# A bidirectional scan's masks in one instruction, its state split at the step's beginning, and the attention gates' SiLU moved into the attention

## The chip, the cores and the metric

One core of a Trainium2 chip runs the whole layer as one program. The metric is the device time of one execution in microseconds (us); smaller is better. The engines are TensorE (PE; PEld is its weight load), VectorE (DVE), ScalarE (ACT), GpSimd (POOL) and SyncE (SP), which issues the transfers here. Each engine takes its instructions in order.

## The reference, cut to what matters

Two sequences, of 512 and 1024 tokens and width 1024, go through one encoder layer. The normalised, modulated input is multiplied by a wide matrix; its columns feed an attention branch and a state-space branch.

```python
branch_a = (attn * jax.nn.silu(gate_a)) @ w_proj_a          # attn: 8 heads, softmax over the sequence
...
CB = jnp.einsum('bclgn,bcsgn->bcgls', Cc, Bc)               # per chunk of 128 and group
Lm = jnp.exp(jnp.where(tri, diff, -jnp.inf))                # decays between two tokens of a chunk
y_diag = jnp.einsum('bcgls,bcgels,bcsgep->bclgep', CB, Lm, xdt)
states = jnp.einsum('bclgn,bclge,bclgep->bcgepn', Bc, decay_states, xdt)
...
y = ssd(x, forward) + flip(ssd(flip(x), backward))          # both directions
merged = sigmoid(g_a) * branch_a + sigmoid(g_b) * (norm(y * silu(z)) @ w_proj_b)
out = x + gate * (merged @ w_out)
```

## The kernel before, in words

All arithmetic is float32. A product that needs precision is made of three matmuls on high and low halves (`mm3`, L88 to L90). A vector over tokens lies as 128 rows by 512 columns; the 1536 tokens are three such windows.

After a first stage (to about 200 us) the kernel goes through four groups `g` of the state-space branch. Each group makes its input projections and convolutions (PE-bound), then its scan, then the `z` gate. A scan is a pre-pass that carries the backward state from the last chunk to the first (`prepass`) and a main pass (`mainpass`) over the 4, then 8 chunks of 128 tokens of the two sequences. A chunk has two steps, `u` = 0 and 1, of four heads each. Between steps `feed` lets PE do parts of the fillers: other projections whose results are wanted later (`qc`, `gate`, `ga`, `gb`; `CUTS` says which group does which). The gate blocks are fillers of the first two groups. A filler's `ev` empties PSUM through ACT (for a gate, through DVE too) into `ft` and stores it.

In a main pass, `head(c)` fetches a chunk's inputs, makes the product of B and C in a PSUM tile `sm` (L651) and two masked copies `cu` of it, for the lower and the upper triangle (L653, L654). `distances` fetches the summed decays `ab`. `weights` subtracts on POOL (L714, two instructions), scales `cu` on ACT (L718, L719), adds (L720), merges the two directions (L721) and takes the exponential (L722). `weigh` multiplies (L727) and `products` does the matmuls (L738). `state` weights the chunk's inputs (L598) and splits them into halves on ACT and POOL (L688 to L691); `follow` multiplies those into the forward state (`mm3`, then L607 and L609). `carried` multiplies both states with C (L677) and scales the result (L678). `tail` adds all up (L743, L744). The PSUM pool `sm` has three slots, which `head`, `follow`, `carried` and the pre-pass take in turn.

The attention follows (about 1600 to 2187 us): 24 units of one head and one window. `scores` does the products of a unit ahead of time (maxima L1017 to L1022, exponentials L1025, whose results are `pp`), `values` transposes and multiplies (L1059, `po`). `gates` turns the sums of the softmax round through memory (`rsD`, `rb`), loads the stored gate `gt` (L1042) and multiplies (L1043); the last step multiplies it by the unit's result (L1072) and stores. `merge` interleaves the lists of these thunks. Fetched weights are cast on ACT (L361) and their low halves made on DVE (L85). The output products end the kernel.

The framework orders each engine's queue itself, from planned durations; the order of the program's text is the priority among the instructions that are ready in that plan.

Of the kernel before, what the change touches and what calls it, by code (L numbers as in the profile page):

```python
# [9 lines left out]
F32 = mybir.dt.float32  # L10
F32R = mybir.dt.float32r
U8 = mybir.dt.uint8
AF = mybir.ActivationFunctionType
ALU = mybir.AluOpType
# [4 lines left out]
P = 128  # L19
T = 1536  # L20
W = 512
# [44 lines left out]
def _body(nc, tc, A, O):  # L66
    V, S, GP, PE = nc.vector, nc.scalar, nc.gpsimd, nc.tensor
# [36 lines left out]
    cmat = const.tile([P, 5, P], F32, name="cmat")  # L104
    nc.sync.dma_start(out=cmat, in_=A["cmat"])
    maskb = const.tile([P, P], U8, name="maskb")
    ident, triF, triB, selL, selF = (cmat[:, i, :] for i in range(5))
# [406 lines left out]
    def filler(kind, i):  # L514
        if kind == "qc":
            def ev(w, ps):
                t = tmp("ft")
                S.copy(t, ps)
                nc.sync.dma_start(out=qcT[i][w], in_=t)
            return inproj_steps(i, ev)  # L520
        elif kind == "gate":
            def ev(w, ps):
                t = tmp("ft")
                S.activation(t, ps, AF.Tanh, scale=0.5)
                V.scalar_tensor_tensor(t, t, 1.0, ps, op0=ALU.add, op1=ALU.mult)
                nc.sync.dma_start(out=sgA[i][w], in_=t)
            return inproj_steps(BLK_GATE + i, ev)
        else:
            dst = tga if kind == "ga" else tgb

            def ev(w, ps):
                t = tmp("ft")
                S.activation(t, ps, AF.Tanh, scale=0.5)
                nc.sync.dma_start(out=dst[i][w], in_=t)
            return inproj_steps((BLK_GA if kind == "ga" else BLK_GB) + i, ev)
# [34 lines left out]
    for g in range(G):  # L570
# [61 lines left out]
        def mainpass(o, n):  # L632
# [5 lines left out]
            def head(c):  # L638
                cs_ = slice(c * P, (c + 1) * P)
                if c == c0:  # L640
                    xb = tok(c, "xb", 2)
                else:
                    xb = pS.tile([P, W + P], F32, name="xb", bufs=2)
                    nc.sync.dma_start(out=xb, in_=xbD[g][c])
                xt, bt = xb[:, :W], xb[:, W:]
                sb = None
                if c < c1 - 1:
                    sb = pS.tile([P, W], F32, name="sb", bufs=2)
                    nc.sync.dma_start(out=sb, in_=sbD[g][c])
                pc = smp.tile([P, P], F32, name="sm")  # L650
                PE.matmul(pc, lhsT=Bt[:, cs_], rhs=Ct[:, cs_], start=True, stop=True)  # L651
                cu = pS.tile([P, 2, P], F32, name="cu", bufs=2)
                V.tensor_tensor(cu[:, 0, :], pc, triF, op=ALU.mult)  # L653
                V.tensor_tensor(cu[:, 1, :], pc, triB, op=ALU.mult)  # L654
                stt[c] = dict(xt=xt, bt=bt, sb=sb, cu=cu)

            def decays(c):
                eb = {}
# [35 lines left out]
            def follow(c):  # L694
                stt[c]["sf"] = sf[0]
                if c < c1 - 1:
                    ps = smp.tile([P, W], F32, name="sm")
                    mm3(ps, *stt[c]["parts"], True, True)
                    sf[0] = advance(sf[0], ps, 0, c, pS.tile([P, W], F32, name="stf", bufs=2))
# [25 lines left out]
            def weigh(c, u):  # L725
                ab, wt = stt[c, u]
                V.tensor_tensor(wt, ab[:, 0], wt, op=ALU.mult)  # L727
                stt[c, u] = wt
# [16 lines left out]

            nu = E // HH
            us = [(c, u) for c in range(c0, c1) for u in range(nu)]
            head(c0)
            for i in range(4):
                xo = xs[i][:, o:o + n]  # L750
# [3 lines left out]
            weights(*us[0])  # L754
            yield
            for i in range(len(us) + 1):
                if i < len(us):
                    weigh(*us[i])
                if i + 2 < len(us):
                    distances(*us[i + 2])  # L760
                if i >= 1:
                    products(*us[i - 1])
                if i < len(us) and us[i][1] == 1:
                    follow(us[i][0])
                    carried(us[i][0])
                if i >= 1 and us[i - 1][1] == nu - 1:
                    tail(us[i - 1][0])
                if i + 1 < len(us):
                    weights(*us[i + 1])
                if i < len(us) and us[i][1] == 0:  # L770
                    c = us[i][0]
                    state(c)
                    decays(c)
                    if c + 1 < c1:
                        head(c + 1)
                yield
# [194 lines left out]
    def scores(u):  # L971

        si, hd, w = u
        o, n = SEQS[si]
        nw = n // W
        h = hd % 2
        st = {}

        def turn_n():
            qrw, qrr, rq, rqn = QR[si, hd // 2, w]  # L980
            nh = p2.tile([P, W], F32R, name="nh", bufs=2)
            nl = p2.tile([P, W], F32R, name="nl", bufs=2)
            pn = spp.tile([P, W], F32, name="sp")
            for b in range(4):
                PE.transpose(out=pn[:, b * P:(b + 1) * P], in_=qrw[:, b, h], identity=ident)
            S.activation(nh, pn, AF.Copy, scale=gqk)
            V.scalar_tensor_tensor(nl, pn, gqk, r32(nh), op0=ALU.mult, op1=ALU.subtract)
            st["n"] = (nh, nl)

        def turn_r():  # L990
            qrw, qrr, rq, rqn = QR[si, hd // 2, w]
            xh = p2.tile([P, W], F32R, name="xh", bufs=2)
            xl = p2.tile([P, W], F32R, name="xl", bufs=2)
            pk = spp.tile([P, W], F32, name="sp")
            for b in range(4):
                PE.transpose(out=pk[:, b * P:(b + 1) * P], in_=qrr[:, b, h], identity=ident)
            S.copy(xh, pk)
            sub(xl, pk, r32(xh))
            st["x"] = (xh, xl)
            PT[u] = []  # L1000
            st["su"] = p2.tile([P, nw, 4], F32, name="su", bufs=4)

        def block(b):
            (nh, nl), (xh, xl) = st["n"], st["x"]
            rq, rqn = QR[si, hd // 2, w][2:]
            bs = slice(b * P, (b + 1) * P)
            sm = p2.tile([P, 8], F32, name="smx", bufs=8)
            sps = []
            for k in range(nw):
                out = spp.tile([P, W], F32, name="sp")  # L1010
                kh, kl, kx = KV[si, hd, k][:3]
                PE.matmul(out, lhsT=nh[:, bs], rhs=kh, start=True, stop=False)  # L1012
                PE.matmul(out, lhsT=nh[:, bs], rhs=kl, start=False, stop=False)  # L1013
                PE.matmul(out, lhsT=nl[:, bs], rhs=kh, start=False, stop=False)  # L1014
                PE.matmul(out, lhsT=xh[:, bs], rhs=kx, start=False, stop=False)  # L1015
                PE.matmul(out, lhsT=xl[:, bs], rhs=kx, start=False, stop=True)  # L1016
                V.reduce_max(sm[:, k:k + 1], out, axis=AX.X)  # L1017
                sps.append(out)
            if nw == 2:
                V.scalar_tensor_tensor(sm[:, 2:3], sm[:, 0:1], sm[:, 1:2], rqn[:, b, h:h + 1], op0=ALU.max, op1=ALU.mult)  # L1020
            else:
                V.tensor_tensor(sm[:, 2:3], sm[:, 0:1], rqn[:, b, h:h + 1], op=ALU.mult)  # L1022
            pp = [p2.tile([P, W], F32, name="pp", bufs=10) for _ in range(nw)]
            for k in range(nw):
                S.activation(pp[k], sps[k], AF.Exp, bias=sm[:, 2:3], scale=rq[:, b, h:h + 1], accum_out=st["su"][:, k, b:b + 1])  # L1025
            PT[u].append(pp)

        def gates():

            su = st["su"]  # L1030
            if nw == 2:
                V.tensor_tensor(su[:, 0], su[:, 0], su[:, 1], op=ALU.add)
            V.reciprocal(su[:, 0], su[:, 0])
            pt = spp.tile([4, P], F32, name="sp")
            PE.transpose(out=pt, in_=su[:, 0], identity=ident)
            rt = p2.tile([4, P], F32, name="rt", bufs=2)
            S.copy(rt, pt)
            nc.sync.dma_start(out=rsD[hd][o // W + w].rearrange("(b q) -> b q", b=4), in_=rt)
            rb = p2.tile([P, W], F32, name="rb", bufs=1)
            nc.sync.dma_start(out=rb, in_=rsD[hd][o // W + w].partition_broadcast(P))  # L1040
            gt = p2.tile([P, W], F32, name="gt", bufs=1)
            nc.sync.dma_start(out=gt, in_=sgA[hd][o // W + w])  # L1042
            GP.tensor_tensor(gt, gt, rb, op=ALU.mult)  # L1043
            GT[u] = gt

        GT[u] = gates
        return [turn_n, turn_r], [lambda b=b: block(b) for b in range(4)]

    def values(u):

# [217 lines left out]
```

## Time and profile before

| | |
|---|---|
| median of 3 runs | 2720.13 us (2719.35 to 2723.41) |
| profiled execution | 2716.42 us |
| its span, first to last instruction | 2714.4 us |
| mean granted TensorE clock | 0.985 of full speed |
| four scans, in windows of 200 us each | 200 to 400, 560 to 760, 920 to 1120, 1320 to 1520 |
| attention | about 1600 to 2187 us |

The profile is one execution. "Busy" is the time in which an engine ran an instruction; matmuls overlap one another, so their single durations are longer than their spacing. A wait is put down to the instruction whose end released it.

### The profile page before, as it was taken

The page shows a single profiled execution, that of the slowest core. Times are in us where ns is not written, and L with a number is a line of the kernel's source. Part 1 is how long each engine was busy: PE and PEld are TensorE (multiplying, and loading weights), DVE is VectorE, ACT ScalarE, POOL GpSimd, SP SyncE. Part 2 cuts the span into 40 slices and gives each one's busy share as a digit, 9 for nine tenths or more (in the row PEclk, how much of TensorE's full clock was granted, in tenths as well). Part 3 has the DMA queues.
Part 4 walks back from the last instruction along what each step waited for, and adds up shares of the span by engine and source line. Part 5 has one row for each costly group of instructions (what it writes and reads, how often), then busy time and mean ns, then how long its engine had stood idle before and what let it go on. Part 6 is the DMA issues. An engine that isn't in the chain of part 4 may idle for free. (4 is left out here: it accounts for less than half of the span.)

```text
span 2714.4 us, 36314 instructions
## 1 busy us (share of the span) xinstructions
PE 2586.5 (95%) x12810; PEld 2080.5 (77%) x12810; DVE 1833.5 (68%) x2962; ACT 1322.6 (49%) x2954; POOL 505.1 (19%) x455
## 2 busy tenths in 40 slices
PE   6999999999999998999998999999999999999999
PEld 2776777877778766878766888888888788888887
DVE  5878785788946678557777568877777753466631
ACT  5545654456624456564556357666665651111210
POOL 1013440023400035110135024322222200000000
PEclk8999999999999999999999999999999999999999
DMA  7227662156722266542466322211110252255433
GB/s 249 77 78 208 187 168 94 39 179 187 207 62 86 82 208 183 136 147 74 146 191 188 92 96 87 84 44 43 34 40 28 71 186 70 78 156 163 128 125 101
DMA packets 211205, 325.86 MB, mean 120 GB/s; under 512 B 24816, under 2 KB 74064, under 8 KB 210256
## 3 DMA queue, kind: packets, MB, share of 16 engines
q1 hardware_dynamic: 211024, 323.55, 39.9%
q8 instruction: 101, 1.65, 0.3%
q14 instruction: 80, 0.66, 0.1%
HBM read 245.56 MB, written 77.91 MB: 119 GB/s over the span
## 5 line engine op out<-in xcount | busy, mean ns | idle before, releaser
L88 PE MATMUL mm<-hH,wh 128*128 128x512 f32 x1656 | 670.2, 405 | 2.3 <-ACT hH L218 2.0
L89 PE MATMUL mm<-hL,wh 128*128 128x512 f32 x1656 | 662.0, 400 | 3.6 <-DVE hL L219 3.6
L90 PE MATMUL mm<-hH,wl 128*128 128x512 f32 x1656 | 653.7, 395 | 1.3 <-DVE wl L85 1.2
L88 PEld LDWEIGHTS mm<-hH,wh 128*128 128x128 f32 x1656 | 314.6, 190 | 84.6 <-issue 14.6
L89 PEld LDWEIGHTS mm<-hL,wh 128*128 128x128 f32 x1656 | 315.4, 190 | 77.3 <-issue 10.2
L90 PEld LDWEIGHTS mm<-hH,wl 128*128 128x128 f32 x1656 | 314.6, 190 | 73.2 <-issue 6.1
L714 POOL TENSOR_TENSOR ab<-ab,dg 128x512 f32<-128x512 f32 x192 | 236.9, 1246 | 418.5 <-DMA ab<-arD 293.4
L88 PE MATMUL mm<-hi,wh 128*128 128x512 f32 x768 | 298.8, 389 | 0.0
L90 PE MATMUL mm<-hi,wl 128*128 128x512 f32 x768 | 298.8, 389 | 0.0
L89 PE MATMUL mm<-lo,wh 128*128 128x512 f32 x768 | 298.8, 389 | 0.0
L85 DVE TENSOR_TENSOR wl<-ws,wh 128x512 fp32r<-128x512 f32 x210 | 151.3, 722 | 134.4 <-ACT wh L226 86.7
L361 ACT CAST wh<-ws 128x512 fp32r<-128x512 f32 x72 | 44.9, 623 | 326.4 <-PE mm L89 311.3
L88 PEld LDWEIGHTS mm<-hi,wh 128*128 128x128 f32 x768 | 144.1, 188 | 30.1
L89 PEld LDWEIGHTS mm<-lo,wh 128*128 128x128 f32 x768 | 144.1, 188 | 29.9
L90 PEld LDWEIGHTS mm<-hi,wl 128*128 128x128 f32 x768 | 144.1, 188 | 29.9
L719 ACT ACTIVATE wt<-cu,dg 128x128 f32<-128x128 f32 x384 | 141.3, 391 | 46.5 <-DVE cu L653 46.1
L1025 ACT ACTIVATE pp<-sp,smx,rq 128x512 f32<-128x512 f32 x160 | 123.6, 777 | 54.9 <-DVE smx L1020 38.8
L361 ACT CAST ph<-tp 128x512 fp32r<-128x512 f32 x160 | 95.3, 598 | 110.4 <-PE tp L1059 110.2
L689 POOL TENSOR_TENSOR btl<-xb,bth 128x128 fp32r<-128x128 f32 x40 | 28.5, 713 | 607.5 <-ACT bth L688 607.4
L563 DVE SCALAR_TENSOR_TENSOR xs<-raw,cwh,xs 128x511 f32<-128x511 f32 (+3 forms) x128 | 129.7, 1021 | 17.5 <-ACT xs L559 14.8
L718 ACT ACTIVATE t<-cu,dg 128x128 f32<-128x128 f32 x384 | 137.3, 390 | 2.6 <-DVE cu L654 2.4
L721 DVE COPY_PREDICATED ab<-maskb,ab 128x512 f32<-128x512 uint8 x96 | 86.4, 905 | 69.3 <-POOL ab L714 69.3
(293 smaller groups left out, 5018.5 us busy)
## 6 DMA issues: line engine op xcount, KB each, us to landing
ab<-arD SPq DMA_DIRECT2D x192, 256.0 KB
ws<-w_in SPq DMA_DIRECT2D x140, 256.0 KB
eb<-arD SPq DMA_DIRECT2D x160, 128.0 KB
xbD<-xp SPq DMA_DIRECT2D x40, 320.0 KB
xb<-xbD SPq DMA_DIRECT2D x40, 320.0 KB
yT<-xs SPq DMA_DIRECT2D x48, 256.0 KB
sg<-yT SPq DMA_DIRECT2D x48, 256.0 KB
tg<-tga SPq DMA_DIRECT2D x48, 256.0 KB
```

Of the source, the lines that this page charges most:

```text
L85: V.tensor_tensor(out, a, b, op=ALU.subtract)
L88: PE.matmul(out, lhsT=ah, rhs=bh, start=first, stop=False)
L89: PE.matmul(out, lhsT=ah, rhs=bl, start=False, stop=False)
L90: PE.matmul(out, lhsT=al, rhs=bh, start=False, stop=last)
L361: S.copy(hi, src)
L563: V.scalar_tensor_tensor(acc[:, lo:hi], raw[:, lo + d:hi + d], cwh[:, 24 + 24 * k + tix:24 + 24 * k + tix + 1], acc[:, lo:hi], op0=ALU.mul ...
L689: GP.tensor_tensor(bl, stt[c]["bt"], r32(bh), op=ALU.subtract)
L714: GP.tensor_tensor(ab[:, d], ab[:, d], ac_[:, d, c, e0:e0 + HH].unsqueeze(2).broadcast_to([P, HH, P]), op=ALU.subtract)
L718: S.activation(t1[:, e], cu[:, 1, :], AF.Copy, scale=dt_[:, 1, c, e0 + e:e0 + e + 1])
L719: S.activation(wt[:, e], cu[:, 0, :], AF.Copy, scale=dt_[:, 0, c, e0 + e:e0 + e + 1])
L721: V.copy_predicated(ab[:, 0], maskb.unsqueeze(1).broadcast_to([P, HH, P]), ab[:, 1])
L1025: S.activation(pp[k], sps[k], AF.Exp, bias=sm[:, 2:3], scale=rq[:, b, h:h + 1], accum_out=st["su"][:, k, b:b + 1])
```

## The change

The two masked copies become one DVE instruction, which reads the product twice through a broadcast and both triangles from the constants. It moves, with the product, into `masks(c)`, called for the next chunk at the beginning of a chunk's first step; `state(c)` moves from the end of that step to its beginning. A gate filler stores the raw projection, copied by ACT. Its SiLU is made in the attention by a new thunk `silu`, the last of a unit's `scores`: it loads the gate, takes the tanh on ACT and does the rest on POOL. The tile `gt` has three buffers where it had one.

```diff
         elif kind == "gate":
             def ev(w, ps):
                 t = tmp("ft")
-                S.activation(t, ps, AF.Tanh, scale=0.5)
-                V.scalar_tensor_tensor(t, t, 1.0, ps, op0=ALU.add, op1=ALU.mult)
+                S.copy(t, ps)
                 nc.sync.dma_start(out=sgA[i][w], in_=t)
...
+                stt[c] = dict(xt=xt, bt=bt, sb=sb, cu=stt[c])
+
+            def masks(c):
+
+                cs_ = slice(c * P, (c + 1) * P)
                 pc = smp.tile([P, P], F32, name="sm")
                 PE.matmul(pc, lhsT=Bt[:, cs_], rhs=Ct[:, cs_], start=True, stop=True)
                 cu = pS.tile([P, 2, P], F32, name="cu", bufs=2)
-                V.tensor_tensor(cu[:, 0, :], pc, triF, op=ALU.mult)
-                V.tensor_tensor(cu[:, 1, :], pc, triB, op=ALU.mult)
-                stt[c] = dict(xt=xt, bt=bt, sb=sb, cu=cu)
+                V.tensor_tensor(cu, pc.unsqueeze(1).broadcast_to([P, 2, P]), cmat[:, 1:3, :], op=ALU.mult)
+                stt[c] = cu
...
+            masks(c0)
             head(c0)
...
             for i in range(len(us) + 1):
+                c, u = us[min(i, len(us) - 1)]
+                begins = i < len(us) and u == 0
+                if begins:
+                    if c + 1 < c1:
+                        masks(c + 1)
+                    state(c)
                 if i < len(us):
-                    weigh(*us[i])
+                    weigh(c, u)
...
-                if i < len(us) and us[i][1] == 0:
-                    c = us[i][0]
-                    state(c)
+                if begins:
                     decays(c)
                     if c + 1 < c1:
                         head(c + 1)
...
+        def silu():
+
+            gt = st["gt"] = p2.tile([P, W], F32, name="gt", bufs=3)
+            nc.sync.dma_start(out=gt, in_=sgA[hd][o // W + w])
+            tg = p2.tile([P, W], F32, name="tgt", bufs=1)
+            S.activation(tg, gt, AF.Tanh, scale=0.5)
+            GP.tensor_tensor(tg, tg, gt, op=ALU.mult)
+            GP.tensor_tensor(gt, tg, gt, op=ALU.add)
+
         def gates():
...
-            gt = p2.tile([P, W], F32, name="gt", bufs=1)
-            nc.sync.dma_start(out=gt, in_=sgA[hd][o // W + w])
+            gt = st["gt"]
             GP.tensor_tensor(gt, gt, rb, op=ALU.mult)
...
-        return [turn_n, turn_r], [lambda b=b: block(b) for b in range(4)]
+        return [turn_n, turn_r], [lambda b=b: block(b) for b in range(4)] + [silu]
```

## Rows read from the trace of the kernel before

**Rows 1.** The page's busy time, share of the span and instructions of each engine

```profile
PE 2586.5 (95%) x12810; PEld 2080.5 (77%) x12810; DVE 1833.5 (68%) x2962; ACT 1322.6 (49%) x2954; POOL 505.1 (19%) x455
```

**Rows 2.** Busy us by windows: the four scans' sum, then the attention

```profile
sum 800.00, PE 734.80 PEld 567.80 DVE 637.71 ACT 470.61 POOL 311.36; mean PE 183.70 PEld 141.95 DVE 159.43 ACT 117.65 POOL 77.84
...
1600.00:2187.00 587.00, 563.07 (x3327) 488.06 (x3326) 451.24 (x994) 376.66 (x959) 165.53 (x168) 1.00 0.18 55
```

**Rows 3.** PE's waits, 200 to 1530 us: total us, times, longest

```profile
PE sm L677 <- DVE cu L654: 21.8, 7, 4.8
PE sm L89 <- POOL zt L691: 14.3, 10, 3.2
PE sm L626 <- DVE eb L678: 9.0, 4, 3.4
...
PE sm L590 <- DVE eb L678: 4.5, 5, 1.3
```

**Rows 4.** Timeline of one step of the third scan: start, us, instruction, idle before

```profile
1070.00 3.48 POOL L714 TENSOR_TENSOR ab<-ab,dg 128x512 f32<-128x512 f32 x2 [6.96 <-DMA ab<-arD]
...
1073.44 0.45 POOL L689 TENSOR_TENSOR btl<-xb,bth 128x128 fp32r<-128x128 f32 x1
...
1073.85 1.71 POOL L691 TENSOR_TENSOR zt<-tmp,zt 128x512 fp32r<-128x512 f32 x1
...
1075.62 0.79 PE L89 MATMUL sm<-zt,bth 128*128 128x512 f32 x1 [3.20 <-POOL zt L691]
...
1082.26 0.68 DVE L744 TENSOR_TENSOR xs<-xs,eb 128x512 f32<-128x512 f32 x1
...
1082.86 0.28 DVE L654 TENSOR_TENSOR cu<-sm,cmat 128x128 f32<-128x128 f32 x1
...
1083.20 1.22 PE L677 MATMUL sm<-ch,sb 128*128 128x128 f32 x4 [4.38 <-DVE cu L654]
```

**Rows 5.** Windows: PE, PEld, DVE, ACT, POOL, clock, DMA; first, last of six, sum

```profile
302.00:318.00 16.00, 13.42 (x65) 10.30 (x65) 13.76 (x19) 8.88 (x25) 8.99 (x9) 0.79 0.63 193
...
1454.00:1474.00 20.00, 12.99 (x46) 10.29 (x43) 14.20 (x19) 9.44 (x25) 11.39 (x11) 0.74 0.62 171
sum 98.00, PE 69.96 PEld 55.52 DVE 81.32 ACT 54.81 POOL 51.50; mean PE 11.66 PEld 9.25 DVE 13.55 ACT 9.14 POOL 8.58
```

**Rows 6.** Groups by line and shape: count | busy us, mean ns | idle before

```profile
L1043 POOL TENSOR_TENSOR gt<-gt,rb 128x512 f32<-128x512 f32 x24 | 31.0, 1293 | 257.0 <-DMA rb<-rsD 217.0 <-DVE smx L1020 16.1 <-DVE qx L889 12.0
...
L85 DVE TENSOR_TENSOR vl<-sp,vh 128x256 fp32r<-128x256 f32 x48 | 19.6, 414 | 0.1
...
L525 DVE SCALAR_TENSOR_TENSOR ft<-ft,mm 128x512 f32<-128x512 f32 x24 | 16.3, 680 | 4.2 <-ACT ft L524 4.2
...
L524 ACT ACTIVATE ft<-mm 128x512 f32<-128x512 f32 x24 | 14.1, 587 | 10.6 <-PE mm L90 10.5
...
L653 DVE TENSOR_TENSOR cu<-sm,cmat 128x128 f32<-128x128 f32 x48 | 13.5, 281 | 0.7 <-PE sm L651 0.7
...
L654 DVE TENSOR_TENSOR cu<-sm,cmat 128x128 f32<-128x128 f32 x48 | 13.3, 278 | 0.0
...
L565 ACT ACTIVATE raw<-xs 128x512 f32<-128x512 f32 x16 | 10.1, 632 | 1.5 <-DVE xs L563 1.1
```

**Rows 7.** PE's waits in the attention, 1600 to 2200 us

```profile
PE tp L1059 <- ACT pp L1025: 4.8, 4, 2.0
...
PE sp L1012 <- ACT pp L1025: 3.5, 5, 0.9
...
PE sp L996 <- POOL qrr L898: 1.8, 1, 1.8
```

**Rows 8.** ACT's groups in the attention, 1600 to 2190 us

```profile
L361 ACT CAST wkh<-stg 128x256 fp32r<-128x256 f32 x30 | 11.9, 428 | 4.2 <-DMA stg<-w_kv 4.2
```

**Rows 9.** The chain that ended last, 2100 to 2140 us: start, us, what

```profile
2132.00 2.68 DMA sg<-yT
```

**Rows 10.** One line of the attention: duration ns, least/median/most

```profile
L1020 DVE SCALAR_TENSOR_TENSOR smx<-smx,rqn x64: 206/220/1325, 1763.5 to 2176.4; 128x1 f32<-128x1 f32 x64
```

## What is predicted

> **What bounds the kernel now.** I read the page's busy line first [rows 1]: TensorE (PE) works 95% of the span, so only what makes PE idle or slow can be won. Next come the windows of the four scans, 800 us in all, and of the attention [rows 2]. In the scans PE is busy 734.8 us, so it idles 65.2 us, and VectorE (DVE) is busy 637.7 us (80%), with GpSimd (POOL) at 39%. In the attention PE idles 587.0 - 563.1 = 23.9 us, ACT is busy 64% of the time and POOL 28%. Elsewhere PE hardly idles.
>
> Then the list of what PE waited for in the scans [rows 3]. The two longest entries are `carried`'s matmuls (L677) waiting for the second mask (L654), 21.8 us, and `follow`'s second matmul (L89) waiting for POOL's low half of the state's input (L691), 14.3 us: 36.1 us of the 65.2. L677 doesn't read the mask. It wants a PSUM slot: the three `sm` slots go round as mask product, `follow`, `carried`, `carried`, so the fourth reuses the mask product's bank and waits until both masks have read it.
>
> The timeline of one bad step [rows 4] shows both. L89 stands 3.20 us until POOL ends L691 (1073.85 to 1075.56), which was queued behind 3.48 us of L714. Then L677 stands 4.38 us, until DVE comes to L654 at 1082.86. The masks' product was on PE long before; DVE reached the masks only after the step's other work, and put L744 ahead of the last one.
>
> Six stretches, 98 us in all, hold the large cases [rows 5]. There PE idles 98.00 - 69.96 = 28.0 us. The granted clock falls too: 0.79 over 16 us, 0.74 over 20 us. Taking (1 - clock) times length over all six gives 18.7 us, at most, that PE loses by slow matmuls after its stalls. The same sum line says DVE was busy 81.3 of the 98 us. The two waits therefore carry at most 36.1 + 18.7 = 54.8 us, and DVE says how much of it can be had.
>
> **The change, part by part.**
>
> Masks: two DVE instructions of 0.281 and 0.278 us become one of 128x256. The nearest row, 128x256 with one PSUM operand, is 0.414 us [rows 6]; bounds are 0.28 (a single mask) and 0.56 (no gain). I take 0.414: 0.145 us less, 48 times, is 7.0 us of DVE.
>
> Gates in the scans: 24 SiLU instructions of 0.680 us leave DVE, 16.3 us, all in the first two scans, where the gate blocks are fillers. On ACT a tanh out of PSUM (0.587 us) becomes a copy out of PSUM of the same size; that tanh is the nearest row, so nothing is counted. The store now waits for ACT alone. Together DVE loses 23.3 of 637.7 us, 3.7%.
>
> Masks and split moved to the step's beginning: no instruction more. PE gets the masks' product before `products`, DVE the masks and the state's weighting (L598) before `weigh`, POOL L689 and L691 before the step's two L714. With the masks read that early, the fourth `sm` slot is free when `carried` asks, and L691 has a step's time before `follow`. So both waits should go. What is late next is DVE itself. In the six stretches DVE would still have 81.3 x 0.963 = 78.3 us to do. If they shrink until DVE is full, they give back 98 - 78.3 = 19.7 us, not 46.7. The waits of the same two kinds outside these stretches are 36.1 - 28.0 = 8.1 us, short and apart, and I count them whole. Gain: 27.8 us. Bounds: 0 if every stall only moves on, 54.8 if DVE's work spreads into its idle 20%; if the lighter DVE also ended PE's waits for L678 [rows 3], 13.5 more.
>
> Attention, ACT: 24 tanh from SBUF at 0.632 us [rows 6] are 15.2 us. ACT's 376.7 us now cost PE 4.8 + 3.5 us of waiting for `pp` [rows 7], 0.022 per us, which prices 15.2 us at 0.3; bounds 0 (ACT idles 36%) and 15.2. No table price is added: L524 and the exponentials already alternate in the scans.
>
> Attention, the load: `gt` is now fetched before the tanh and ACT, which works in order, waits for it with the exponentials and casts of the softmax behind it. The nearest case is ACT's casts of fresh weights, fetched by the same queue: 30 of them waited 4.2 us in all [rows 8], 0.14 each. For 24 that is 3.4 us; the upper bound is a whole fetch each, 2.68 us as for `sg` [rows 9], or 64 us. I take 3.4, because the load needs nothing but a free buffer out of three and can be issued ahead. It also no longer waits for the previous store of the only `gt` buffer.
>
> Attention, POOL: 48 instructions of 1.293 us [rows 6] are 62 us on an engine with 421 us idle. POOL's 165.5 us cost PE 1.8 us [rows 7], so 62 cost 0.7; bounds 0 and 62.
>
> A small DVE instruction, the scaled maximum L1020, takes 0.22 us as a median but up to 1.325 [rows 10]. With 62 of 587 us more of POOL, 7 of its 64 more might be caught so, at most 7.7 us of DVE, and hidden, as DVE idles 23% here. The Trainium skill (SBUF — State Buffer, "Who interferes with whom") gives a reason to fear more: a DVE instruction with two SBUF inputs and a GpSimd instruction that reads SBUF exclude each other, for the whole instruction. The long L1020 fits that; by this rule alone the sum would be up to 7.7 us higher, by the idle DVE it is unchanged.
>
> Sum: 27.8 won, 0.3 + 3.4 + 0.7 = 4.4 lost, 23.4 us net. The profiled execution took 2716.4 us (span 2714.4), giving 2693.0. The runs' median, 2720.1, lies 3.7 above the profiled execution, so the forecast is **2697 us**; its own range is 2686 to 2708.
>
> **The rivals.**
>
> *Everything goes.* PE gets all 54.8 us: 2720.1 - 54.8 + 4.4 = 2670, and 2656 if the L678 waits end too. For it: DVE idles a fifth of the scans, and the earlier masks also let ACT start the weights (L718, L719) earlier. Against it: 81.3 of 98 us busy where it matters.
>
> *Handed on.* The masks' product now stands early in PE's own queue and wants the `sm` slot of the `follow` before; PE waits there for DVE's L609, or in `products` for L727, as long as it used to wait later. Only the scattered 8.1 us remain: 2720.1 - 8.1 + 4.4 = 2716. For it: DVE is nearly full in the stretches. Against it: 0.145 and 0.68 us instructions really go, and the fillers lie between.
>
> *Slower, by the fetch.* If each tanh stands a whole 2.68 us for its `gt` and PE stands too, 64.3 us replace the 3.4: 2697 + 60.9 = 2758. It decides (slower by 0.2%) from (27.8 - 1.0 + 5.4) / 24 = 1.34 us a unit. Against it stand the 0.14 us of rows 8.
>
> *Slower, by POOL's order in the scans.* L689 and L691, 0.45 + 1.71 us in rows 4, now go ahead of the L714 pair in each of 40 chunks, (4 - 1) + (8 - 1) in each of 4 groups; L721, the exponential, `weigh` and `products` are behind them. If nothing hides it, 40 x 2.16 = 86.4 us: 2783. It decides from (23.4 + 5.4) / 40 = 0.72 us a chunk. Against it: POOL idles 61% of the scans, and the next step's L714 stood behind these two anyway.
>
> **How the numbers follow.** Chances: forecast 0.50; everything goes 0.17; handed on 0.20; fetch 0.07; POOL's order 0.06. What a measurement here can tell from no change is about 0.2%, 5.4 us. Faster takes the first two and about half of "handed on", whose 2716 lies just inside the bound: 0.76. Same is 0.09. Slower, the last two with the bad end of "handed on": 0.15. The range starts at 2660, inside the best rival, and ends at 2722, beyond "handed on"; the two slower rivals and the best end of the best one stay out, about 0.18.
>
> **What would show it.** Right: L677 no longer waits for a mask, one mask row of about 0.41 us x48, L89's wait for L691 near nothing, PE's idle in the scans near 40 us and the clock there nearer 1; DVE's scan total down by 23 us. In the attention 24 tanh near 0.63 us with little waiting on `gt`, POOL up by some 62 us, PE's idle 24 to 30 us. Wrong: a new wait of PE on L651 or L738 of the old size, a longer wait of L721 for L714, or ACT standing before the tanh.

## The result, and the profile after

The changed kernel took 2735.1 us (median of 4 runs, 2731.46 to 2739.72) against 2719.74 us for the kernel before beside it: ratio 1.0066, interval 1.0050 to 1.0083. It is slower, and outside the predicted range. Its profiled execution took 2733.86 us, span 2732.0, clock 0.981.

Most lines have moved. In the kernel after, the masks' product is L655 (was L651) and the mask L657; `carried` is L680 and L681 (L677, L678); the state's weighting is L597 (L598), its split L691 to L694 (L688 to L691); `advance` is L606 and L608 (L607, L609); the load of `xb` is L643 (L644), of `eb` L666 (L663), of `ab` L709 (L706); POOL's subtraction is L717 (L714), the weights L721 to L723, the merge L724 (L721), `weigh` L730 (L727), `products` L741 (L738), `tail` L746 (L743). In the attention the tanh is L1041 and POOL's two are L1042 and L1043.

The page's busy line of the kernel after, beside [rows 1]:

```profile
PE 2590.4 (95%) x12810; PEld 2086.1 (76%) x12810; DVE 1832.8 (67%) x2890; ACT 1337.9 (49%) x2978; POOL 565.1 (21%) x503
```

DVE has 72 instructions fewer (24 of the SiLU and 48 masks), yet is busy only 0.7 us less; below is why. The windows of the kernel after, columns as in [rows 2] and [rows 5] (clock third from the end): the four scans, their sum, the attention. The windows are fixed in time, and the kernel after runs up to 20 us behind the kernel before in them; lengths by stage follow below.

```profile
200.00:400.00 200.00, 175.94 (x950) 136.45 (x949) 157.62 (x213) 115.63 (x313) 79.89 (x69) 0.97 0.67 192
560.00:760.00 200.00, 181.12 (x958) 140.28 (x958) 157.91 (x211) 117.82 (x316) 79.39 (x67) 0.95 0.69 194
920.00:1120.00 200.00, 179.33 (x923) 139.55 (x922) 151.53 (x204) 115.80 (x302) 71.79 (x61) 0.94 0.62 175
1320.00:1520.00 200.00, 178.24 (x942) 138.57 (x943) 155.33 (x215) 118.06 (x316) 74.44 (x62) 0.96 0.63 181
sum 800.00, PE 714.62 PEld 554.85 DVE 622.39 ACT 467.31 POOL 305.52; mean PE 178.65 PEld 138.71 DVE 155.60 ACT 116.83 POOL 76.38
...
1600.00:2187.00 587.00, 567.75 (x3312) 490.13 (x3311) 457.26 (x989) 391.13 (x974) 224.52 (x214) 1.00 0.20 60
```

PE idles 800 - 714.6 = 85.4 us in the scans, where it idled 65.2; in the attention 587 - 567.8 = 19.3 us, where it idled 23.9 [rows 2]. So the loss is in the scans. The list of waits of the kernel after, 200 to 1530 us (total, times, longest), for PE, DVE and the transfers' queue on SP (SPq), beside [rows 3]:

```profile
PE sm L655 <- DVE stf L608: 28.7, 6, 7.2
PE sm L680 <- DVE cu L657: 12.5, 8, 3.0
...
DVE tmp L597 <- DMA xb<-xbD: 17.8, 7, 4.9
...
SPq L643 <- PE py L741: 31.3, 11, 5.6
SPq L666 <- DVE eb L683: 31.2, 20, 5.4
```

L89's wait for POOL has gone from the list, and `carried`'s for the mask fell from 21.8 to 12.5 us. But the masks' product itself now stands 28.7 us for `advance`, and DVE waits for the input `xb` 17.8 us in 7 waits, where it waited 6.2 us in 2. SP, before it issues the load of `xb`, waits 31.3 us for `products` to free the buffer, where it waited 12.9. The same rows of the kernel before:

```profile
DVE tmp L598 <- DMA xb<-xbD: 6.2, 2, 4.2
...
SPq L644 <- PE py L738: 12.9, 8, 3.0
```

The timeline of one bad step of the first scan (start, us, instruction, idle before and its releaser) shows how they hang together:

```profile
365.53 3.63 SPq L666 DMA_DIRECT2D eb<-arD  x3
...
368.53 0.69 DVE L730 TENSOR_TENSOR wt<-ab,wt 128x512 f32<-128x512 f32 x1
369.26 0.55 SPq L643 DMA_DIRECT2D xb<-xbD  x1
...
372.97 0.69 DVE L597 TENSOR_TENSOR tmp<-xb,dg 128x512 f32<-128x512 f32 x1 [3.74 <-DMA xb<-xbD]
373.58 0.68 DVE L608 TENSOR_TENSOR stf<-stf,sm 128x512 f32<-128x512 f32 x1
...
374.31 0.80 PE L655 MATMUL sm<-ch,kd 128*128 128x128 f32 x2 [7.21 <-DVE stf L608]
```

Read it from the top. SP is at the loads of `eb` from 365.53, and issues that of `xb` behind them at 369.26. DVE has come to L597, the weighting of the chunk that begins, and stands 3.74 us until `xb` lands. Behind L597 in DVE's queue is L608, which needs none of it: it adds up the chunk before and would free its `sm` slot. The moved masks' product L655 is at the head of PE's queue and wants that slot: PE stands 7.21 us. The same pattern stands at 735.44 (PE idle 6.26 us), 1116.73 (4.97) and 1502.65 (5.54). Each of the four is the last masks' product of its scan, and together they are 24.0 of the 28.7 us.

The clock pays too. Windows of that step, before and after the stall, columns as above:

```profile
362.00:367.00 5.00, 5.00 (x36) 4.02 (x34) 3.37 (x7) 3.10 (x11) 2.95 (x3) 1.00 0.52 148
374.00:378.00 4.00, 3.69 (x15) 2.75 (x16) 4.00 (x7) 2.07 (x7) 3.72 (x3) 0.50 0.54 173
```

After 7.21 us without a matmul the granted clock is at 0.50, the lower level of 1.2 GHz, where it was at 2.4.

For where the time went, each profile was cut into stages: a scan is from a group's first transpose of the chunks to its last matmul of `products`; "between" is the sum of the three stretches from one scan to the next; "attention" is from the last scan's end to the first copy of an output product. All in us.

| kernel | scans 1 to 4 | sum | between | attention | span |
|---|---|---|---|---|---|
| before | 187.0, 191.9, 201.7, 197.7 | 778.3 | 532.5 | 683.7 | 2714.4 |
| after | 192.8, 200.8, 203.1, 201.6 | 798.3 | 532.0 | 681.3 | 2732.0 |

The span grew by 17.6: 20.0 more in the scans and 0.5 ahead of them, less 2.4 in the attention and 0.5 between.

### The profile page after: what moved, and what is told of

Its sections match the earlier page's. It is cut to its first block, busy times and chain, and to the rows that moved or that the text cites. A ratio compares the mean times of both kernels' runs of the same rounds, so it can differ in the third digit from the quotient of the medians.

```text
span 2732.0 us, 36345 instructions
## 1 busy us (share of the span) xinstructions
PE 2590.4 (95%) x12810; PEld 2086.1 (76%) x12810; DVE 1832.8 (67%) x2890; ACT 1337.9 (49%) x2978; POOL 565.1 (21%) x503
## 4 chain that ended last, share of the span: by engine, by line
PE 72%; DVE 10%; DMA 8%; ACT 4%; issue 3%; POOL 2%; SPq 1%; DVEq 0%; ACTq 0%; POOLq 0%
PE mm L88 17%; PE mm L90 17%; PE mm L89 17%; DMA ab<-arD 3%; PE tp L1075 2%; DMA eb<-arD 2%; PE sp L90 1%; PE sp L89 1%; PE sp L88 1%; PE sp L1020 1%; PE sp L1021 1%; PE po L88 1%; PE sp L1023 1%; PE sp L1024 1%; PE sp L1022 1%
## 5 line engine op out<-in xcount | busy, mean ns | idle before, releaser
L89 PE MATMUL mm<-hL,wh 128*128 128x512 f32 x1656 | 660.8, 399 | 2.2 <-DVE hL L219 2.2
L89 PEld LDWEIGHTS mm<-hL,wh 128*128 128x128 f32 x1656 | 316.2, 191 | 76.2 <-issue 8.8
L717 POOL TENSOR_TENSOR ab<-ab,dg 128x512 f32<-128x512 f32 x192 | 235.3, 1234 | 439.7 <-DMA ab<-arD 301.0
L89 PE MATMUL mm<-lo,wh 128*128 128x512 f32 x768 | 298.8, 389 | 0.0
L361 ACT CAST wh<-ws 128x512 fp32r<-128x512 f32 x72 | 44.8, 622 | 325.5 <-PE mm L89 310.8
L89 PEld LDWEIGHTS mm<-lo,wh 128*128 128x128 f32 x768 | 144.2, 188 | 29.9
L721 ACT ACTIVATE t<-cu,dg 128x128 f32<-128x128 f32 x384 | 144.6, 394 | 32.6 <-DVE cu L657 30.9
L724 DVE COPY_PREDICATED ab<-maskb,ab 128x512 f32<-128x512 uint8 x96 | 88.3, 920 | 73.4 <-POOL ab L717 73.4
L226 ACT CAST wh<-ws 128x512 fp32r<-128x512 f32 x138 | 84.2, 615 | 105.1 <-PE mm L89 101.2
```

The source lines that it names most:

```text
L89: PE.matmul(out, lhsT=ah, rhs=bl, start=False, stop=False)
L226: S.copy(a, ws)
L717: GP.tensor_tensor(ab[:, d], ab[:, d], ac_[:, d, c, e0:e0 + HH].unsqueeze(2).broadcast_to([P, HH, P]), op=ALU.subtract)
L721: S.activation(t1[:, e], cu[:, 1, :], AF.Copy, scale=dt_[:, 1, c, e0 + e:e0 + e + 1])
L724: V.copy_predicated(ab[:, 0], maskb.unsqueeze(1).broadcast_to([P, HH, P]), ab[:, 1])
```

## Experiments

The theories: **late input** (A in the expectations): the moved weighting meets an input that is issued late, and what is queued behind it frees a slot late. **Early masks** (B): the masks' product, moved ahead on PE, makes PE stand by itself. **DVE's load** (D): a lighter DVE shortens the scans, a heavier one lengthens them. And the gates' part may cost time by itself (G); or the single mask instruction, with the order that the planner makes of it, does (M). A filler's DVE step may also help by where it stands in the queues, and by the PSUM bank that it holds (O). Diffs are against the kernel after, if nothing else is said. Ratios are to the kernel before on the same chip. These runs were on other chips than the result's, where the kernel before took 2708.5 to 2708.9 us, so its profile was taken there again.

**State back, masks early**

```diff
                 if begins:
                     if c + 1 < c1:
                         masks(c + 1)
-                    state(c)
...
                 if begins:
+                    state(c)
                     decays(c)
```

> Theory A: the state's weighting (L597), moved to the step's beginning, stands in DVE's queue for the chunk's input, which SP fetches late; L608 behind it frees the PSUM slot late, and PE stands before the masks' product (L655). Theory B: the masks' product, moved early, asks for follow's slot too early whatever the state does. Here the state goes back to the end of the first step and the masks stay early. A: DVE's wait for the input falls from 17.8 us to under 8, PE's wait before the masks' product from 28.7 us to under 10, time 2700 to 2715 us. B: the 28.7 us stay above 20, time about 2730 us.

Measured: 1.0002, interval 0.9985 to 1.0019. The list of waits of this kernel, 200 to 1530 us, for PE:

```profile
PE sm L89 <- POOL zt L694: 16.3, 15, 2.0
PE sm L655 <- DVE stf L608: 13.6, 6, 3.7
PE sm L680 <- DVE cu L657: 11.5, 4, 3.4
```

DVE's wait for `xb` isn't there any more, L655's is halved (13.6 us; I had set under 10), and L89's for POOL is back at its old size [rows 3]. The whole loss is gone with one line.

**Masks back, state early**

```diff
                 if begins:
-                    if c + 1 < c1:
-                        masks(c + 1)
                     state(c)
...
                     if c + 1 < c1:
+                        masks(c + 1)
                         head(c + 1)
```

> The masks go back to the end of the first step, still as one instruction, and the state stays at its beginning. A: DVE still waits some 15 us for the chunk's input, PE's idle time moves to another instruction behind it, time 2720 to 2740 us. B: PE's wait before the masks' product falls under 5 us and the time to 2700 to 2715 us.

Measured: 1.0104, interval 1.0077 to 1.0132, the slowest of all. Early masks are not the cause; without them it is worse. Its waits, 200 to 1560 us:

```profile
DVE tmp L597 <- DMA xb<-xbD: 26.3, 15, 3.9
PE sm L655 <- DVE stf L608: 20.3, 7, 5.5
PE sm L680 <- DVE cu L657: 17.6, 7, 4.7
PE sm L589 <- DVE eb L681: 17.3, 5, 4.5
```

**Both back, one mask instruction and the gates' part kept.** Both edits above together.

> Masks and state both at their old places; the masks in one instruction and the gates' SiLU in the attention stay. Both theories: neither wait appears, PE waits for the masks in carried and for POOL's half in follow as before, some 36 us, and the time is that of the kernel before less what a DVE lighter by 23 us gives and what the attention gives: 2705 to 2720 us. If the time is 2730 us again, neither move is the cause, and it is the gates or the planner's order.

Measured: 1.0027, interval 1.0012 to 1.0042. With it the four make a square:

| | state late | state early |
|---|---|---|
| masks late | 1.0027 | 1.0104 |
| masks early | 1.0002 | 1.0066 |

The early state costs 0.0077 and 0.0064, the early masks win 0.0025 and 0.0038; all four have the gates' part in them. The kernel with both moves undone is in the range that I had set (2717.0 us), but it has DVE's lighter work and is still slower than the kernel before, clear of its interval. So the lighter DVE won nothing there. DVE's wait for `xb`, at the old place of the state, is 10.6 us in it.

**The whole change, the chunk's input issued before the decays**

```diff
                 if begins:
-                    decays(c)
                     if c + 1 < c1:
                         head(c + 1)
+                    decays(c)
```

> All of the change stays, but the next chunk's input is issued before the decays, so that it doesn't stand behind them in SP's queue. A: DVE's wait for the input falls from 17.8 us to under 6, PE's wait before the masks' product from 28.7 us to under 12, time 2705 to 2718 us. B: both stay, time about 2730 us or more.

Measured: 0.9989, interval 0.9972 to 1.0005. No arithmetic is changed, only the priority of the loads of `xb` and `sb` against those of `eb`, and the loss is gone. Its waits, 200 to 1530 us:

```profile
PE sm L680 <- DVE cu L657: 15.8, 8, 4.3
...
PE sm L655 <- DVE stf L608: 7.0, 4, 3.6
...
DVE tmp L597 <- DMA xb<-xbD: 1.9, 3, 0.8
```

`xb` 17.8 to 1.9 us, and with it L655 from 28.7 to 7.0. This is the direct test of the late input, and it holds. The engines' queues stayed nearly as they were: matched in order by line and tile against the kernel after, at least 96% of the instructions of PE, DVE, ACT and POOL in the first 180 us of each scan stand in the same order (99% between the two profiles of the kernel after). So it isn't a new order of the engines that won it back.

**The two halves of the change alone, and both kernels again.** The gates' part added to the kernel before; the scan's part alone (the kernel after with L524, L525 and `gates` of before); the kernel after again; a profile of the kernel before.

> Only the gates' part of the change, on the kernel before: the fillers copy, the SiLU is made in the attention. With both moves undone the kernel was still 1.0027 of the time before. Theory G: the gates' part costs that, although it takes 16 us from DVE: ratio 1.002 to 1.004. Theory M: the single mask instruction and the order that the planner makes of it cost it: ratio 0.996 to 1.000.

> Only the scan's part: one mask instruction, masks and state at the step's beginning; the gates as before. Theory A (the late input) says that the whole loss is here: ratio 1.006 or more, DVE waiting 15 us or more for the chunk's input. If the gates cost 0.3%, as theory G has it, the ratio is 1.003 to 1.005; if their lighter DVE helped in the first two scans, 1.008 or more.

> The changed kernel itself, beside the others of this call: its ratio was 1.0066 on another chip, and the other kernels' ratios are compared with it. Both theories: 1.005 to 1.009.

> The kernel before, for a profile from the same chip as the three above: stage lengths are compared with this one. Both theories: scans of 187, 192, 202 and 198 us, within 3 us each; if they differ by more, stage lengths from different chips can't be set beside each other.

Measured: gates' part 1.0021 (1.0007 to 1.0036), scan's part 1.0031 (1.0016 to 1.0047), after again 1.0063 (1.0039 to 1.0087); the profile of before has a span of 2701.7 us. The halves add up, 0.0021 + 0.0031 = 0.0052 of 0.0063, within the intervals. But theory A had the whole loss in the scan's part, 1.006 or more with 15 us of waiting for `xb`, and that fell: it is half of the loss, with 9.2 us. With the masks early in both, the early state alone costs 0.0038 without the gates' part (0.9993, below, to 1.0031) and 0.0064 with it. The stages:

| kernel | scans 1 to 4 | sum | span |
|---|---|---|---|
| before, again | 183.4, 190.2, 198.3, 194.8 | 766.7 | 2701.7 |
| after, again | 190.9, 201.0, 201.7, 199.3 | 792.9 | 2724.9 |
| gates' part alone | 188.5, 195.3, 197.6, 195.9 | 777.3 | 2712.0 |
| scan's part alone | 186.7, 193.7, 199.0, 198.7 | 778.1 | 2710.6 |
| input before decays | 185.1, 193.9, 195.4, 195.7 | 770.1 | 2702.0 |
| useless step, below | 186.0, 191.8, 190.7, 188.3 | 756.8 | 2692.1 |
| useless step in the gates' part, below | 188.1, 189.7, 201.4, 194.5 | 773.7 | 2709.2 |

The first four are from one chip, the fifth from another, the last two from a third. The kernel before is up to 3.7 us a scan from what I had expected of it, where 3 was the bound for comparing chips, so stage lengths of different chips can't be set beside each other closely. Also, its profiled execution here (2703.67 us) was 5 us under its median on this chip, so differences to it come out too large by about that. Again the scans lose it all: 26.2 us, the span 23.2, of which the medians bear out 20. The gates' part is 5.1 us longer in each of the first two scans, the ones whose DVE it makes lighter, and 0.4 us in the other two together; of these 10.6 us the medians bear out 6.8.

**Masks early alone.** The kernel before with `masks`, in one instruction, at the beginning; state and gates as before.

> Of the change only the masks: one instruction, at the step's beginning. State and gates as before. From the runs so far the early masks are worth -0.25% (1.0002 against 1.0027 with the gates' part in both) and the gates' part +0.2%. If these add up: ratio 0.997 to 0.999. If the masks' gain was one with the gates' lighter DVE, 1.000 to 1.002.

Measured: 0.9993, interval 0.9982 to 1.0003. In its list of waits (200 to 1560 us) the wait that the masks' move was to end is half gone, and one of the same size stands in its place:

```profile
PE sm L656 <- DVE stf L609: 23.1, 8, 5.1
...
PE sm L681 <- DVE cu L658: 10.8, 4, 3.1
```

The kernel before, on a later chip, had:

```profile
PE sm L677 <- DVE cu L654: 21.1, 7, 5.4
...
PE sm L651 <- DVE stf L609: 3.7, 3, 1.7
```

21.1 us for the mask became 10.8, 3.7 us for `advance` became 23.1. PE asks for an `sm` slot once more ahead of what frees it. The wait was handed on, and nothing that can be told from noise came of it; 0.9993 lies between the two ranges that I had set.

**The scan's part alone, the input before the decays**

> The scan's part whole (masks and state early) with the next chunk's input issued before the decays; gates as before. If the late input is the whole trouble of the early state and the gates' 0.2% adds up: ratio 0.996 to 0.998. If the early state costs something besides, 1.000 to 1.002.

Measured: 0.9992, interval 0.9981 to 1.0004; 0.0039 less than the scan's part. That lies between the two ranges that I had set, but the mend works without the gates' part too, and nothing beyond it can be told. The gates' part can now be priced in four pairs, without and with it: 1.0000 and 1.0021; scan's part 1.0031 and 1.0063; masks early alone 0.9993 and 1.0002; input first 0.9992 and 0.9989. It costs something where the old and the late inputs are, and nothing that can be told where the masks alone are early or the input is mended.

**Useless DVE work.** To the kernel before, in the evacuation of the `ga` and `gb` fillers (third and fourth group), a DVE step that leaves the values as they are; and, in the gates' part alone, the same step in place of the one that it removed:

```diff
                 t = tmp("ft")
                 S.activation(t, ps, AF.Tanh, scale=0.5)
+                V.scalar_tensor_tensor(t, ps, 0.0, t, op0=ALU.mult, op1=ALU.add)
                 nc.sync.dma_start(out=dst[i][w], in_=t)
```

> The kernel before with one more DVE instruction of 0.68 us in each evacuation of a ga or gb filler, which reads PSUM and leaves the values as they are (t + 0 * ps). Theory D: DVE's load holds the scans back, so 33 us more of it make the third and fourth scans longer, ratio 1.002 to 1.006. Theory O: the scans with the gate fillers lost 5 us each when that DVE step went, since the step holds the filler's PSUM bank and sets the order and spacing of PE's queue; then the third and fourth scans get shorter by some 5 us each, ratio 0.996 to 0.998.

> The gates' part alone, with a DVE instruction of the same size left in the gate fillers (copy by ACT, then t + 0 * ps on DVE). Theory D: DVE has its old load and nothing is won back from the 1.0021, ratio 1.002 or more. Theory O: the first two scans take their old lengths, 183 and 190 us, and the ratio falls to 0.999 to 1.001.

Measured: 0.9966 (0.9952 to 0.9980), faster; and 1.0000 (0.9984 to 1.0016). The third and fourth scans, in windows of 200 us each: first the kernel before on a later chip, then the kernel with the useless step.

```profile
918.00:1118.00 200.00, 183.62 (x969) 141.25 (x968) 158.84 (x224) 117.70 (x315) 71.83 (x62) 0.96 0.64 190
1304.00:1504.00 200.00, 183.60 (x987) 142.42 (x986) 160.44 (x241) 118.52 (x316) 73.66 (x62) 0.97 0.65 190
```

```profile
918.00:1118.00 200.00, 186.94 (x1007) 144.97 (x1006) 171.61 (x247) 120.21 (x319) 74.73 (x62) 0.98 0.64 192
1304.00:1504.00 200.00, 188.23 (x1016) 146.46 (x1015) 178.18 (x268) 120.82 (x321) 74.07 (x62) 0.99 0.64 194
```

The step added 32 us to DVE's busy time (1871.2 against 1839.3 us on the page). DVE is busy 12.8 and 17.7 us more in these windows, and PE 3.3 and 4.6 us more. The two scans are 7.6 and 6.5 us shorter than in the kernel before on its chip, and 10.7 and 6.2 us shorter than in the gates' part with the step kept, on the same chip. So DVE's load isn't what sets the length of these scans. In the gates' part with the step kept, the ratio is as theory O has it; of the first two scans, the second took its old length (189.7) and the first, at 188.1, did not. DVE's wait for POOL's subtraction fell, in the lists of waits of the same two kernels, 200 to 1560 us:

```profile
DVE ab L721 <- POOL ab L714: 60.3, 33, 6.0
```

```profile
DVE ab L722 <- POOL ab L715: 36.5, 21, 4.2
```

That this wait is what was won isn't shown: in the combination below it is 41.8 us, and the time is 0.9990.

**Is it the PSUM bank that the step holds, and does it add to the mended scan?** The same step reading only `t`, so that ACT alone frees the bank; and the step, reading PSUM, added to the scan's part with the input first.

```diff
-                V.scalar_tensor_tensor(t, ps, 0.0, t, op0=ALU.mult, op1=ALU.add)
+                V.scalar_tensor_tensor(t, t, 0.0, t, op0=ALU.mult, op1=ALU.add)
```

> The kernel before, and in the ga and gb fillers' evacuation a DVE step that leaves the values as they are and reads only the SBUF tile, so that ACT alone frees the PSUM bank. The 33 us of DVE work and the later store are those of the run with the filler step that read PSUM (0.9966). If the bank held longer was the help: 1.000 (0.998 to 1.002). If the step's place in the queues, or the later store, was the help: 0.9966 again (0.995 to 0.9985). If DVE's load were what limits: 1.005 or more.

> The scan's part of the change with the chunk's input issued before the decays, gates as before, and the DVE step that reads PSUM in the ga and gb evacuation. If the two helps add: 0.9992 x 0.9966 = 0.9958 (0.994 to 0.9975). If both feed on the same stalls: 0.9966 to 0.999, no better than either alone.

Measured: 0.9984 (0.9970 to 0.9997), inside both ranges that I had set, for the bank and for the queues, and its interval overlaps that of the step that reads PSUM: undecided between the two. It again speaks against DVE's load. The combination: 0.9990 (0.9977 to 1.0003), so they don't add. Its masks' product waits 29.7 us for `advance`. The fastest version is the kernel before with the useless step, 0.9966.

**The profiles side by side.** The time goes with DVE's wait for `xb`. In 200 to 1530 us it is 8.9 us or more in each of the six profiles whose ratio is clear above 1 (8.9 gates' part, 10.6 both moves undone, 9.2 scan's part, 15.3 and 17.8 the kernel after, 26.3 masks back), and 6.2 or less in all others. PE's wait for `advance` before the masks' product doesn't sort them so. First the scan's part alone (1.0031), then the combination (0.9990), then the gates' part alone (1.0021):

```profile
PE sm L656 <- DVE stf L609: 29.7, 8, 5.7
DVE tmp L598 <- DMA xb<-xbD: 9.2, 3, 3.5
```

```profile
PE sm L657 <- DVE stf L610: 29.7, 8, 5.9
```

```profile
DVE tmp L597 <- DMA xb<-xbD: 8.9, 4, 3.2
```

In the combination the wait for `xb` is 4.5 us. This is a correlation of profiles; the cause is tested only where the load was moved.

## Why the prediction was wrong

**What was read of the kernel before** held: the two waits were there again on a later chip, 21.1 and 11.6 us. The changed kernel was forecast faster and came out 0.66% slower.

**The step that failed** is "Masks and split moved to the step's beginning: no instruction more", costed at nothing, with "So both waits should go. What is late next is DVE itself." I counted what the moved `state` issues and not what it waits for. `head` asks for a chunk's input at the end of the chunk before's first step; the old place of the weighting comes two steps later, the new one only one. DVE's wait for it rose to 17.8 us, and PE stood 28.7 us for what was queued behind. And SP issues that load late: it stands 31.3 us in all for `products` to free the buffer, and behind loads of `eb` that wait 31.2 us for DVE. The row was in reach: DVE already waited for `xb` 6.2 us in 2 waits, up to 4.2 us, in the trace of before, and the chunk's input is the last thing that a first step issues. The cost is shown by the square (0.0064 and 0.0077, 17 to 21 us of 2709; 0.0038 without the gates' part) and by the priority of that load (1.0066 to 0.9989; 1.0031 to 0.9992 without the gates' part).

**A second step failed**, "Gates in the scans": 16.3 us taken from DVE were counted as a gain. Alone, the gates' part made the kernel 0.21% slower (5.7 us). Why is open, see below.

**The gain of 27.8 us** failed too, by itself. It was made of a lighter DVE and of two waits that end. The masks early alone, with the lighter DVE that goes with them, gave 0.9993; with the state early and its input mended, 0.9992. Their intervals leave it about 5 us at most. "Handed on" named this mechanism, PE standing at the masks' product for L609, which came with 28.7 us, but priced it as if the queue behind DVE could add nothing. The point that I held against it, that DVE's removed 23 us are relief, fell: the kernel with both moves undone and the lighter DVE took 1.0027, and 32 us of useless DVE work made the kernel faster.

**The terms of the sum**, beside [rows 6]: groups by line and shape of the kernel after (count, busy us, mean ns, idle before).

```profile
L657 DVE TENSOR_TENSOR cu<-sm,cmat 128x256 f32<-128x256 f32 x48 | 19.9, 414 | 11.9 <-PE sm L655 11.9
...
L1041 ACT ACTIVATE tgt<-gt 128x512 f32<-128x512 f32 x24 | 15.2, 633 | 15.7 <-DMA gt<-sgA 10.3 <-POOL gt L1043 5.1
...
L524 ACT COPY ft<-mm 128x512 f32<-128x512 f32 x24 | 13.8, 574 | 12.3 <-PE mm L90 12.3
...
L1042 POOL TENSOR_TENSOR tgt<-tgt,gt 128x512 f32<-128x512 f32 x24 | 31.3, 1305 | 130.2 <-ACT tgt L1041 103.5 <-DVE pl L85 19.2 <-DVE ssq L891 7.5
```

The mask is 0.414 us, as taken; the tanh 0.633 against 0.632; POOL's instruction 1.305 against 1.293, and POOL's busy time grew by 60.0 us against 62. ACT stood 10.3 us for `gt` where 3.4 were taken, but PE didn't stand for it: the attention cost nothing, against 4.4 us. From the last scan's end to the first output product it took 681.3 us, before 683.7. Right durations didn't help, because the path wasn't where they were removed.

**DVE's total** is down by 0.7 us and not by 23.3. The work removed is what it was said to be (16.3 of SiLU, and 26.8 of masks became 19.9). Summed over single durations DVE is down by 6.8 us, so the other instructions took 16.4 longer, among them L723, 79.3 us before and 84.6 after; the rest is that neighbouring instructions overlap (above, L597 starts at 372.97 and takes 0.69 us, and L608 starts at 373.58), so that taking one out frees less than its duration. Cut at the stages of the table, DVE is down by 7.9 us in the scans and up by 7.3 in the attention (by the fixed windows, 15.3 and 6.0). That this comes near the bound of 7.7 is luck: the instruction that the bound was made for, the scaled maximum, got shorter. Before, then after:

```profile
L1020 DVE SCALAR_TENSOR_TENSOR smx<-smx,rqn 128x1 f32<-128x1 f32 x64 | 27.9, 435 | 2.0
```

```profile
L1028 DVE SCALAR_TENSOR_TENSOR smx<-smx,rqn 128x1 f32<-128x1 f32 x64 | 20.9, 327 | 1.6
```

Two other groups of the attention in the kernel after, and the second of them before:

```profile
L85 DVE TENSOR_TENSOR vl<-sp,vh 128x256 fp32r<-128x256 f32 x48 | 19.5, 414 | 0.1
L85 DVE TENSOR_TENSOR wkl<-stg,wkh 128x256 fp32r<-128x256 f32 x30 | 17.3, 585 | 3.8 <-ACT wkh L361 3.6
```

```profile
L85 DVE TENSOR_TENSOR wkl<-stg,wkh 128x256 fp32r<-128x256 f32 x30 | 12.6, 427 | 0.1
```

`wkl`, both inputs in SBUF, took 427 ns before; `vl`, one input in PSUM, is at 414 as it was [rows 6]. The Trainium skill (SBUF — State Buffer, "Who interferes with whom") says that VectorE and GpSimd share a pair of SBUF ports and that one locks the other out; the pair `vl` and `wkl` agrees with it, now that POOL is busier (225 us of the attention's window, 166 before). The scaled maximum, with both inputs in SBUF too, went from 435 to 327 ns, so a busier POOL doesn't lengthen every such instruction. No cost of it was seen in the time of the attention.

**The other rivals.** The fetch: 10.3 us of ACT's waiting, none of PE's; far from 64. POOL's order in the scans: DVE's wait for L717 was 72.5 us after and 68.4 before (L721 for L714), so the split ahead of the subtraction cost little. "Everything goes" had nothing of it.

**What stays open.** Why the gates' part costs 0.2%, and why a useless DVE step helps. With that step kept in the gates' evacuation the ratio is 1.0000, but the intervals of 1.0000 and 1.0021 overlap. A rival isn't excluded: the order that the planner gives PE. Matched by line and tile against the kernel before on the later chip, the queues of the useless step's kernel are the same in the first two scans (98% and more of PE's instructions, as between the two profiles of the kernel before), but in the third and fourth, which got shorter, only 77% of PE's instructions match. In the gates' part it is 68% in the second scan. In the first, 97% match, and its 188.5 us can't be told from scatter: with PE's order of before, that scan took from 182.1 us (the step that reads only SBUF) to 188.1 (the step kept). So whether the step helps by the bank, by its place or by the order that it makes isn't shown. The gates' part also has the longer wait for `xb` (8.9 us against 6.2 and 3.2 in the two profiles of the kernel before); why `xb` is later there wasn't tested. A third buffer for `xb` wasn't tried.

## What to carry to other kernels

When an instruction is moved forward in an engine that works in order, look up when each of its inputs is issued and lands at the new place, and what queued behind it frees a slot that another engine waits for; a load's place in its queue has to move with its first reader. A wait for a slot of a ring is ended by freeing the slot earlier, not by asking for it earlier: the request in front only takes the wait with it. An engine that is busy 80% beside a stalled one isn't thereby the limit: put useless work on it before counting its relief as a gain, and look whether the queues kept their order, since a planner that orders them anew is a rival explanation.
